# A five-unit decoder layer on one core: PSUM banks copied out at once, convolution taps tied to each pair, two operations moved to VectorE, first loads reordered

## The chip, the core and the metric

The kernel runs on one core of a Trainium2 chip. The core has a matrix engine (TensorE, PE in the rows, with its weight loads as PEld), VectorE (DVE), ScalarE (ACT), GpSimd (POOL) and SyncE (SP), whose queue (SPq) issues every DMA of this kernel. Each engine takes its own instructions in the order in which the program lists them. The metric is device time of the whole program in microseconds.

## What is computed

One mixer layer over 4096 rows of 1024 numbers, all in fp32:

```
h    = layer_norm(x)
proj = h @ w_in                          # 1024 -> 3072, split in six parts of 512
a    = a_val * sigmoid(a_gate)
y_a  = silu(layer_norm(causal_depthwise_conv(a, 31 taps))) * silu(a_z)
v    = layer_norm(gelu(b_v));  sv = masked 128x128 W_s per head @ v + b_s
y_b  = gelu(b_u) * sv * silu(b_z)
mix  = concat(y_a, y_b) @ w_out          # 1024 -> 1024
h    = layer_norm(2**0.25 * h + mix)
out  = h + sigmoid(h @ w_gate + b) * (p @ w_ple)
```

## The kernel before

**Units and pairs.** The five matrix products of 1024 by 1024 are five *units*, run one after the other. Unit 0 makes `a`, unit 1 makes `u` and `v` and the spatial mix, unit 2 makes the two `silu` gates, unit 3 is the output projection with its residual and norm, unit 4 the gate and the result. A unit walks over 16 *pairs* of 128 rows each. What a unit leaves for a later one goes to DRAM (`hT`, `qD`, `aD`, `cD`, `uD`, `ybD`, `azD`, `zT`).

**One pair.** A pair is a 2 by 2 block product done with seven products in place of eight (`group`, L320; the order is 1, 5, 6, 3, 7, 2, 4). A product is 12 matmuls of 512 columns, because each operand is split in a high and a low part and three of the four combinations are kept (`product`, L304). So a pair has 84 such matmuls. The partial sums live in four PSUM banks of one buffer each, with tags A, B, D and E. Bank B is used by products 1, 6 and 7 one after the other; between them an instruction reads it (`plus`, L323, on ACT in units 0 to 2 and on DVE at L327 or L329 in units 3 and 4). Product 2 adds to bank A and product 4 to bank D, and both banks are first written by a `plus`: `pa` and `pd`. What a pair makes in halves `c12` and `c22` comes from `tt(to12, ...)` (L345) and `tt(to22, ...)` (L350) on DVE. Two more banks (tag S) serve transposes, two (tag acc) the convolution.

**Left operands.** They are made one pair ahead: in units 0, 3 and 4 from 16 transposes and seven splits (`rows_left`, L242), in units 1 and 2 from the `qD` kept by unit 0 (`left_kept`, L232). A split (`left`, L226) is a copy on ACT and a subtraction on POOL or DVE.

**Weights.** Seven weight operands of a unit are split by `split_weight` (L168) on ACT and DVE. Those of units 1 to 4 are made in DRAM (`twD`) during the unit before by `combos` (L176: loads, 16 POOL subtractions, stores) and loaded in that unit's last pair (`load_operands`, L406), since their 14 buffers are those of the running unit.

**Background work.** Between products, `between(i)` (i from 0 to 5) advances five lists of generators: left operands (`bg`), weights (`bg_w`), rows two pairs ahead (`bg_x`), the work after a pair (`bg_post`) and the convolution (`bg_conv`). The convolution has 16 pieces (4 blocks of 1024 rows by 4 channel groups), each of 47 DVE instructions, the *taps* (L379, L381, L387, L390), 752 in all. A block becomes available when unit 0 has made its four pairs; `y_rows` (unit 3's input) needs it. The number of taps per `between` is the last argument of `unit`: 2 in unit 0, 3 in units 1 and 2, 2 in unit 3.

**The order on an engine.** The program is written in this order, but a planner then lays out each engine's list from planned times, and may put an instruction of a background list ahead of where it is written when its engine would be free. The order is fixed at build time.

**Buffers.** SBUF tiles of up to 8 KB per partition share one pool of seven (`big`): rows, staged weights, `hr`, `y`, `cz`, `z`, and the broadcast rows `eb`, `prow`, `gb`. A new tile waits for one of the seven.

**Where the change lies.** In unit 3 the norm of a pair (`body_d`, L687) reads bank A and bank D by `moments` (L147, L148, DVE), takes the power and the bias on POOL (`scale_bias`, L154) and only then is the bank read for the last time:

```python
for dst, src in ((z[:, j, 0:C], ps), (z[:, j, C:], z[:, j, C:])):
    act(dst, src, ID, scale=mv[:, 0, 1:2], bias=nb[:, 0:1])
```

`y_rows` (L636) does the same with a bank of tag S. `norm_v` (L573, unit 1) scales and shifts `v` with two POOL operations, L580 and L581. `first_operands` (L200) issues the eight loads of the first weights after the first rows are normed; `gb`, the gate's bias (L738), is loaded after unit 3 has ended.

## Time and profile before

| what | value |
|---|---|
| median of 3 runs | 2052.64 us (2052.59 to 2060.61) |
| the profiled execution: its own time | 2056.51 us |
| the profiled execution: its span | 2054.8 us, mean granted clock 0.955 |
| units 0 to 4, from the ends of their last products | 414.4, 375.6, 331.2, 481.9 and 451.8 us |

Times in the rows are microseconds from the first instruction unless marked ns. The granted clock is TensorE's, as a share of 2.4 GHz. In rows of single instructions, what stands in brackets is how long the engine stood idle before it and what ended that. In rows of stretches, each engine has its busy time and its number of instructions.

### The profile page before, as it was taken

The page shows a single profiled execution, that of the slowest core. Times are in us where ns is not written, and L with a number is a line of the kernel's source. Part 1 is how long each engine was busy: PE and PEld are TensorE (multiplying, and loading weights), DVE is VectorE, ACT ScalarE, POOL GpSimd, SP SyncE. Part 2 cuts the span into 40 slices and gives each one's busy share as a digit, 9 for nine tenths or more (in the row PEclk, how much of TensorE's full clock was granted, in tenths as well). Part 3 has the DMA queues.
Part 4 walks back from the last instruction along what each step waited for, and adds up shares of the span by engine and source line. Part 5 has one row for each costly group of instructions (what it writes and reads, how often), then busy time and mean ns, then how long its engine had stood idle before and what let it go on. Part 6 is the DMA issues. An engine that isn't in the chain of part 4 may idle for free.

```text
span 2054.8 us, 24446 instructions
## 1 busy us (share of the span) xinstructions
PE 1857.2 (90%) x8322; PEld 1504.2 (73%) x8322; DVE 1354.9 (66%) x2139; ACT 869.9 (42%) x1406; POOL 1361.2 (66%) x1110
## 2 busy tenths in 40 slices
PE   4798999988899998999999787889888699999999
PEld 3687888867687886788887566667666477888887
DVE  7648999999999999884004434444446565666665
ACT  4654555653354545444446323333333422223331
POOL 2869877468888887886665666655556545566661
PEclk8999999999999999999999988999998899999999
DMA  6579676766634436995457475333334422222221
GB/s 221 195 257 321 236 245 205 251 210 210 217 117 145 127 121 222 325 353 201 174 190 273 157 253 208 125 122 144 130 126 153 170 93 85 86 87 88 88 93 57
DMA packets 184926, 363.63 MB, mean 177 GB/s; under 512 B 49633, under 2 KB 74209, under 8 KB 177121
## 3 DMA queue, kind: packets, MB, share of 16 engines
q1 hardware_dynamic: 184800, 362.07, 51.1%
q8 instruction: 66, 1.08, 0.2%
q14 instruction: 60, 0.48, 0.1%
HBM read 211.02 MB, written 150.99 MB: 176 GB/s over the span
## 4 chain that ended last, share of the span: by engine, by line
PE 63%; DMA 10%; DVE 9%; POOL 8%; ACT 4%; issue 4%; SPq 0%; DVEq 0%; POOLq 0%; ACTq 0%
PE pb L309 9%; PE pb L310 8%; PE pb L311 8%; PE pe L309 5%; PE pe L310 5%; PE pe L311 5%; PE pp L764 4%; PE tp L254 3%; PE pa L309 3%; PE pa L310 3%; PE pa L311 3%; POOL alo L229 2%; PE pd L309 2%; PE pd L311 2%; PE pd L310 2%
## 5 line engine op out<-in xcount | busy, mean ns | idle before, releaser
L309 PE MATMUL pb<-whi,ahi 128*128 128x512 f32 x960 | 404.4, 421 | 96.8 <-DVE pa L329 48.1
L229 POOL TENSOR_TENSOR alo<-s,ahi 128x512 fp32r<-128x512 f32 x192 | 261.5, 1372 | 322.5 <-ACT ahi L228 311.8
L310 PE MATMUL pb<-wlo,ahi 128*128 128x512 f32 x960 | 394.6, 411 | 1.1 <-DVE wlo L173 1.1
L311 PE MATMUL pb<-whi,alo 128*128 128x512 f32 x960 | 393.7, 410 | 1.7 <-DVE alo L229 1.7
L309 PEld LDWEIGHTS pb<-whi,ahi 128*128 128x128 f32 x960 | 192.1, 200 | 147.9 <-DVE pa L329 52.4
L309 PE MATMUL pe<-whi,ahi 128*128 128x512 f32 x640 | 257.9, 403 | 9.9 <-ACT ahi L228 5.4
L311 PE MATMUL pe<-whi,alo 128*128 128x512 f32 x640 | 255.9, 400 | 6.4 <-POOL alo L229 6.4
L310 PE MATMUL pe<-wlo,ahi 128*128 128x512 f32 x640 | 254.0, 397 | 5.8 <-DVE wlo L173 5.8
L229 POOL TENSOR_TENSOR alo<-qa,ahi 128x512 fp32r<-128x512 f32 x128 | 165.5, 1308 | 96.9 <-ACT ahi L228 95.5
L311 PEld LDWEIGHTS pb<-whi,alo 128*128 128x128 f32 x960 | 191.6, 200 | 44.9 <-DVE alo L229 2.4
L310 PEld LDWEIGHTS pb<-wlo,ahi 128*128 128x128 f32 x960 | 192.1, 200 | 41.5 <-DVE wlo L173 3.7
L381 DVE SCALAR_TENSOR_TENSOR acc<-ca,cs_sb,acc 128x512 f32<-128x512 f32 x240 | 180.2, 751 | 4.6
L390 DVE SCALAR_TENSOR_TENSOR acc<-ca,cw_sb,acc 128x512 f32<-128x512 f32 x240 | 179.2, 747 | 0.2
L228 ACT ACTIVATE ahi<-s 128x512 fp32r<-128x512 f32 x192 | 120.1, 630 | 125.4 <-DVE s L281 60.1
L387 DVE SCALAR_TENSOR_TENSOR acc<-zy,cw_sb,acc 128x512 f32<-128x512 f32 x224 | 167.1, 746 | 1.2
L229 DVE TENSOR_TENSOR alo<-tp,ahi 128x512 fp32r<-128x512 f32 x144 | 98.7, 685 | 95.5 <-ACT ahi L228 89.9
L309 PEld LDWEIGHTS pe<-whi,ahi 128*128 128x128 f32 x640 | 122.3, 191 | 37.8 <-ACT ahi L228 7.9
L229 POOL TENSOR_TENSOR alo<-qb,ahi 128x512 fp32r<-128x512 f32 x96 | 126.4, 1328 | 32.3 <-ACT ahi L228 31.0
L311 PEld LDWEIGHTS pe<-whi,alo 128*128 128x128 f32 x640 | 122.3, 191 | 33.4 <-POOL alo L229 8.4
L310 PEld LDWEIGHTS pe<-wlo,ahi 128*128 128x128 f32 x640 | 122.3, 191 | 32.2 <-DVE wlo L173 8.3
L309 PE MATMUL pd<-whi,ahi 128*128 128x512 f32 x320 | 129.5, 405 | 5.1 <-ACT pd L325 5.1
L228 ACT ACTIVATE ahi<-tp 128x512 fp32r<-128x512 f32 x144 | 84.8, 590 | 105.7 <-PE tp L254 104.8
(149 smaller groups left out, 4001.7 us busy)
## 6 DMA issues: line engine op xcount, KB each, us to landing
qa<-qD SPq DMA_DIRECT2D x32, 1024.0 KB, 6.6
twD<-bq SPq DMA_DIRECT2D x112, 256.0 KB, 5.4
wst<-twD SPq DMA_DIRECT2D x28, 1024.0 KB, 5.8
qb<-qD SPq DMA_DIRECT2D x32, 768.0 KB, 6.9
xr<-in_x SPq DMA_DIRECT2D x32, 512.0 KB, 5.0
hT<-xr SPq DMA_DIRECT2D x32, 512.0 KB, 3.0
qD<-s SPq DMA_DIRECT2D x64, 256.0 KB, 3.2
bq<-in_wq SPq DMA_DIRECT2D x64, 256.0 KB, 5.3
```

The costliest lines, as they stand in the source:

```text
L228: act(hi, src, ID)
L229: eng.tensor_tensor(lo, src, hi.bitcast(F32), op=SUB)
L254: nc.tensor.transpose(out=tp[:, kk * P : (kk + 1) * P], in_=rows[:, j, k * P : (k + 1) * P], identity=ident,)
L309: nc.tensor.matmul(ps, lhsT=ah[:, k, :], rhs=wh[:, k, :], start=start and k == 0, stop=False, **kw)
L310: nc.tensor.matmul(ps, lhsT=ah[:, k, :], rhs=wl[:, k, :], start=False, stop=False, **kw)
L311: nc.tensor.matmul(ps, lhsT=al[:, k, :], rhs=wh[:, k, :], start=False, stop=k == 3, **kw)
L381: stt(even, src, w, even, op0=MUL, op1=ADD)
L387: stt(dst, src, cw_sb[:, ct, 2 * k + 1 : 2 * k + 2], odd if k else even, op0=MUL, op1=ADD)
L390: stt(src if k == NE - 1 else even, src, cw_sb[:, ct, 2 * k : 2 * k + 1], even, op0=MUL, op1=ADD,)
L764: nc.tensor.matmul(pp, lhsT=l[:, k, ts], rhs=r[:, k, cs], start=k == 0 and l is ph and r is wp_hi, stop=k == 1 and l is pl,)
```

## The change

The diff has these parts.

1. Unit 3's norm: ACT copies banks A and D to `z` as soon as they are done, and a new generator `z_out` makes the moments, the scale and the store from SBUF in the next pair, as `bg_post` steps.
2. The same in `y_rows`: the transposed convolution is copied out of its bank first, the two norms share one `scale_bias` call.
3. `group` records in `anchor` the last of L345 and L350; convolution taps are advanced only at `between(2)` and `between(3)`, and `tc.issue_after` keeps each tap behind that instruction in DVE's list. Quotas go from 2, 3, 3, 2 at six places to 6, 6, 10, 5 at two places.
4. Unit 1's scale and shift of `v` go from POOL (`ptt`) to DVE (`tt`).
5. The loads of the first weights are issued before the first rows are normed; `gb` is loaded in unit 3's last pair.

```diff
--- before.py
+++ after.py
@@ -197,13 +197,16 @@
             dma(twD[u][ROW[4]][:, c], q[:, 2])
             yield
 
-    def first_operands(W):
+    def load_first():
         stg = {}
         for ij in ((0, 0), (0, 1), (1, 1), (1, 0)):
             stg[ij] = big([P, 4, C], "wst")
             for c in range(2):
                 cs = slice(2 * c, 2 * c + 2)
                 dma(stg[ij][:, cs], wq[0][ij][:, cs])
+        return stg
+
+    def first_operands(W, stg):
         b11, b12, b22, b21 = (stg[ij] for ij in ((0, 0), (0, 1), (1, 1), (1, 0)))
 
         def sub(dst, a, b):
@@ -316,6 +319,8 @@
         nc.gpsimd.memset(z.bitcast(F32), 0.0)
         for tag in ("A", "D"):
             nc.tensor.matmul(pbank(tag, "seed"), lhsT=z[:, 0, :], rhs=flat(z), start=True, stop=True)
+
+    anchor = []
 
     def group(L, W, add, to12, to22, between, scale=None):
 
@@ -342,12 +347,12 @@
         plus(u2, pb, 1)
         between(1)
         product(pe, 3, L, W, False)
-        tt(to12, pe, u2, op=ADD)
+        anchor[:] = [tt(to12, pe, u2, op=ADD)]
         between(2)
         product(pb, 7, L, W, False)
         pd = pbank("D", "pd")
         plus(pd, pb, 2)
-        tt(to22, pb, s5, op=ADD)
+        anchor[:] = [tt(to22, pb, s5, op=ADD)]
         between(3)
         product(pa, 2, L, W, False)
         between(4)
@@ -437,7 +442,9 @@
                     bg_w.step(2 if i == 5 else 1)
                 else:
                     bg_w.step(1)
-                bg_conv.step(conv_quota)
+                if i in (2, 3):
+                    with tc.issue_after(anchor[0].ins):
+                        bg_conv.step(conv_quota)
 
             body(p, L, W, between)
             bg.drain()
@@ -474,13 +481,14 @@
     load_x(0)
     W = {}
     eb = broadcast(erow, 2, "eb")
+    stg = load_first()
     for _ in h_rows(0, nc.vector):
         pass
     open_banks()
     L = {}
     for _ in rows_left(L, X.pop(0), qD[0]):
         pass
-    first_operands(W)
+    first_operands(W, stg)
     dma(cw_sb, cw)
     nc.vector.tensor_copy(cs_sb, cw_sb[:, :, 0::2])
     tt(cs_sb[:, :, 0 : NE - 1], cs_sb[:, :, 0 : NE - 1], cw_sb[:, :, 1::2], op=ADD)
@@ -529,7 +537,7 @@
         bg_post.drain()
         bg_post.add(a_out(p, (c12, c22)))
 
-    L, W = unit(0, L, W, left_a, lambda L: left_kept(0, L), body_a, 2, 2)
+    L, W = unit(0, L, W, left_a, lambda L: left_kept(0, L), body_a, 2, 6)
     bg_post.drain()
 
 
@@ -577,8 +585,8 @@
             moments([v], mv[:, 0, :])
             nb = scale_bias(mv)
             act(v, v, ID, scale=mv[:, 0, 1:2], bias=nb[:, 0:1])
-            ptt(v, v, sgb[0][:, 0], op=MUL)
-            ptt(v, v, sgb[1][:, 0], op=ADD)
+            tt(v, v, sgb[0][:, 0], op=MUL)
+            tt(v, v, sgb[1][:, 0], op=ADD)
             act(V["h"][:, i], v, ID)
             ptt(V["l"][:, i], v, V["h"][:, i].bitcast(F32), op=SUB)
 
@@ -598,7 +606,7 @@
         if p % 2 == 1:
             bg_post.add(mix(p // 2, V["g"], V["h"], V["l"]))
 
-    L, W = unit(1, L, W, left_kept, lambda L: left_kept(0, L), body_b, 2, 3)
+    L, W = unit(1, L, W, left_kept, lambda L: left_kept(0, L), body_b, 2, 6)
     bg_post.drain()
 
 
@@ -646,11 +654,16 @@
                     in_=cc[:, ct, j],
                     identity=ident,
                 )
-            mv = mvtile(1)
-            moments([tp], mv[:, 0, :])
-            nb = scale_bias(mv)
+            act(y[:, j, 0:C], tp, ID)
+        yield
+        mv = mvtile(2)
+        for j in (1, 0):
+            moments([y[:, j, 0:C]], mv[:, j, :])
+        nb = scale_bias(mv)
+        yield
+        for j in (1, 0):
             ya = y[:, j, 0:C]
-            act(ya, tp, ID, scale=mv[:, 0, 1:2], bias=nb[:, 0:1])
+            act(ya, ya, ID, scale=mv[:, j, 1:2], bias=nb[:, j : j + 1])
             yield
             ptt(ya, ya, cgb[0][:, 0], op=MUL)
             ptt(ya, ya, cgb[1][:, 0], op=ADD)
@@ -678,11 +691,24 @@
             cgb.append(broadcast(crow[i : i + 1, :], 1, "cgb", utile))
         yield from first_y(L)
 
-    L, W = unit(2, L, W, left_kept, first_y_, body_c, 2, 3)
+    L, W = unit(2, L, W, left_kept, first_y_, body_c, 2, 10)
 
 
     for _ in y_rows(1):
         pass
+
+    def z_out(p, z):
+        mv = mvtile(2)
+        for j in range(2):
+            moments([z[:, j, 0:C], z[:, j, C:]], mv[:, j, :])
+            yield
+        nb = scale_bias(mv)
+        yield
+        yield
+        for j in range(2):
+            act(z[:, j], z[:, j], ID, scale=mv[:, j, 1:2], bias=nb[:, j : j + 1])
+            dma(zT[p][j], z[:, j])
+            yield
 
     def body_d(p, L, W, between):
         if p == 1:
@@ -698,12 +724,9 @@
             z[:, 0, C:], z[:, 1, C:], between, scale=ALPHA,
         )
         for j, ps in ((0, pa), (1, pd)):
-            mv = mvtile(1)
-            moments([ps, z[:, j, C:]], mv[:, 0, :])
-            nb = scale_bias(mv)
-            for dst, src in ((z[:, j, 0:C], ps), (z[:, j, C:], z[:, j, C:])):
-                act(dst, src, ID, scale=mv[:, 0, 1:2], bias=nb[:, 0:1])
-            dma(zT[p][j], z[:, j])
+            act(z[:, j, 0:C], ps, ID)
+        bg_post.drain()
+        bg_post.add(z_out(p, z))
 
     Z = {}
 
@@ -719,14 +742,16 @@
             ptt(Z[p][:, j], Z[p][:, j], pb_[0][:, 1], op=ADD)
             yield
 
-    pb_ = []
+    pb_, last_const = [], []
 
     def first_z(L):
         pb_.append(broadcast(prow, 2, "prow"))
+        last_const.append(broadcast(grow, 1, "gb")[:, 0])
         yield from z_rows(0)
         yield from rows_left(L, Z[0])
 
-    L, W = unit(3, L, W, left_y, first_z, body_d, 2, 2)
+    L, W = unit(3, L, W, left_y, first_z, body_d, 2, 5)
+    bg_post.drain()
 
 
     wp_hi, wp_lo = big([P, 2, D], "wph", F32R), big([P, 2, D], "wpl", F32R)
@@ -735,7 +760,7 @@
     for k in range(2):
         act(wp_hi[:, k], wps[:, k], ID)
         tt(wp_lo[:, k], wps[:, k], wp_hi[:, k].bitcast(F32), op=SUB)
-    gb = broadcast(grow, 1, "gb")[:, 0]
+    gb = last_const[0]
     for _ in z_rows(1):
         pass
```

## Rows read from the trace of the kernel before

**Rows 1.** The profile's first table: each engine's busy time, share of the span and number of instructions.

```profile
PE 1857.2 (90%) x8322; PEld 1504.2 (73%) x8322; DVE 1354.9 (66%) x2139; ACT 869.9 (42%) x1406; POOL 1361.2 (66%) x1110
```

**Rows 2.** Busy time by stretch: unit 0's first pair, the rest of unit 0, then units 1, 2, 3 and 4. Columns: the stretch, its length, each engine's busy time and number of instructions, granted clock, DMA share, GB/s.

```profile
0.00:76.00 76.00, 39.00 (x123) 26.96 (x124) 56.25 (x71) 35.99 (x46) 30.32 (x28) 0.84 0.57 201
76.00:414.00 338.00, 332.13 (x1612) 273.22 (x1612) 276.84 (x447) 194.71 (x321) 255.68 (x185) 0.99 0.73 252
414.00:790.00 376.00, 342.16 (x1510) 277.31 (x1508) 355.65 (x599) 178.99 (x309) 320.89 (x298) 0.97 0.50 162
790.00:1121.00 331.00, 320.36 (x1385) 261.25 (x1385) 164.32 (x225) 155.74 (x249) 231.12 (x178) 0.97 0.71 251
1121.00:1603.00 482.00, 399.54 (x1743) 319.06 (x1741) 229.69 (x442) 171.73 (x270) 280.40 (x297) 0.90 0.46 163
1603.00:2055.00 452.00, 423.97 (x1957) 346.39 (x1955) 272.16 (x360) 132.77 (x216) 242.84 (x127) 0.97 0.26 90
```

**Rows 3.** The same for the convolution's taps on DVE alone, in units 0, 1 and 2 (no other stretch has any). Columns: the stretch, its length, DVE busy time in taps and their number, granted clock, DMA share, GB/s.

```profile
76.00:414.00 338.00, 138.50 (x193) 0.99 0.73 252
414.00:790.00 376.00, 286.12 (x405) 0.97 0.50 162
790.00:1121.00 331.00, 108.32 (x154) 0.97 0.71 251
```

**Rows 4.** Busy time by stretch as in rows 2, finer: unit 1's pairs 0 to 5 and 6 to 15; unit 2's pairs 7 to 14 (to 1102); unit 3's pairs 0 to 4 and 5 to 14; one pair of unit 0 (pair 10); one pair of unit 3 (pair 7).

```profile
414.00:575.00 161.00, 135.50 (x561) 107.04 (x560) 152.62 (x246) 71.47 (x121) 131.32 (x120) 0.93 0.64 207
575.00:790.00 215.00, 206.66 (x951) 170.28 (x949) 203.03 (x355) 107.52 (x189) 189.56 (x179) 1.00 0.40 129
950.00:1102.00 152.00, 152.00 (x676) 126.00 (x675) 13.96 (x24) 67.07 (x112) 93.32 (x73) 1.00 0.52 186
1121.00:1290.00 169.00, 132.85 (x564) 103.34 (x562) 76.39 (x145) 58.68 (x93) 106.92 (x110) 0.89 0.62 211
1290.00:1576.00 286.00, 243.01 (x1080) 196.63 (x1079) 131.01 (x273) 102.81 (x163) 159.12 (x181) 0.92 0.37 133
284.00:306.00 22.00, 22.00 (x110) 18.19 (x109) 19.98 (x33) 12.71 (x21) 17.95 (x15) 1.00 0.72 246
1348.00:1376.00 28.00, 23.70 (x109) 19.20 (x108) 12.88 (x27) 10.03 (x16) 15.56 (x19) 0.94 0.35 129
```

**Rows 5.** Waits over the whole run: who waited for what, the total in us, how often, the longest. L579 is an instruction of unit 1 alone, L329 of unit 3 alone.

```profile
ACT v L579 <- POOL nb L161: 44.5, 16, 7.9
...
PE pb L309 <- DVE pa L329: 48.1, 16, 3.6
```

**Rows 6.** The instructions in order of time around the start of unit 3's pair 10: start, duration, engine, line, operation. The first row reads bank A for the moments; the last four are single matmuls of the product after the wait.

```profile
1437.53 0.68 DVE L147 BATCH_NORM_STATS2 st<-pa 128x6 f32<-128x512 f32 x1
...
1441.91 0.74 POOL L161 TENSOR_SCALAR nb<-mv 128x1 f32<-128x1 f32 x3
...
1443.49 0.77 ACT L705 ACTIVATE z<-pa,nb,mv 128x512 f32<-128x512 f32 x1
...
1444.29 0.70 DVE L329 SCALAR_TENSOR_TENSOR pa<-hr,pb 128x512 f32<-128x512 f32 x1 [2.03 <-ACT z L705]
...
1445.04 0.79 PE L309 MATMUL pb<-whi,ahi 128*128 128x512 f32 x1 [3.61 <-DVE pa L329]
...
1446.06 0.63 PE L311 MATMUL pb<-whi,alo 128*128 128x512 f32 x1
1446.49 0.63 PE L309 MATMUL pb<-whi,ahi 128*128 128x512 f32 x1
...
1448.41 0.39 PE L311 MATMUL pb<-whi,alo 128*128 128x512 f32 x1
1448.64 0.39 PE L309 MATMUL pb<-whi,ahi 128*128 128x512 f32 x1
```

**Rows 7.** Groups of instructions of one line and shape over the whole run: number, busy time in us, mean ns of one, idle time of the engine before them.

```profile
L580 POOL TENSOR_TENSOR v<-v,sgb 128x512 f32<-128x512 f32 x32 | 42.2, 1329 | 3.9 <-ACT v L579 3.6
L769 DVE TENSOR_TENSOR zr<-zr,c 128x512 f32<-128x512 f32 x32 | 53.9, 1683 | 1.1
L769 DVE TENSOR_TENSOR zr<-zr,sg 128x512 f32<-128x512 f32 x32 | 22.1, 692 | 1.1
L259 ACT ACTIVATE zq<-tp 128x512 f32<-128x512 f32 x64 | 38.0, 595 | 45.6 <-PE tp L254 43.0 <-DMA aD<-at 2.4
L468 ACT ACTIVATE xr<-xr,nb,mv 128x1024 f32<-128x1024 f32 x32 | 38.5, 1239 | 17.3 <-POOL nb L161 17.1
```

**Rows 8.** A piece of the chain of work that ended last, inside unit 1's pair 3: start, length, what.

```profile
505.33 8.28 DMA twD<-bq
```

**Rows 9.** The instructions in order of time around unit 4's first pair, columns as in rows 6.

```profile
1619.24 0.38 SPq L416 DMA_DIRECT2D gb<-in_grow  x1
...
1623.75 0.70 DVE L327 TENSOR_TENSOR pa<-pb,gb 128x512 f32<-128x512 f32 x1 [1.62 <-DMA gb<-in_grow]
...
1624.60 0.76 PE L309 MATMUL pb<-whi,ahi 128*128 128x512 f32 x1 [18.73 <-DVE pa L327]
```

**Rows 10.** The same at the program's start.

```profile
14.72 1.46 SPq L471 DMA_DIRECT2D hT<-xr  x2
...
16.22 2.39 SPq L206 DMA_DIRECT2D wst<-in_wq  x4
...
21.42 1.06 ACT L172 ACTIVATE whi<-wst 128x1024 fp32r<-128x1024 f32 x1 [0.92 <-DMA wst<-in_wq]
```

## The prediction, made before the change was run

> **What bounds the kernel now.** I read the engine table first. PE is busy for 90% of the span and no other engine for more than 66% [rows 1], so the time is made of PE's work and of the places where PE waits or runs slowly. The stretches by unit show where those are [rows 2]: the granted clock is 0.97 to 0.99 in most units, 0.84 in the first pair and 0.90 in unit 3. The finer stretches give a yardstick [rows 4]. A pair of unit 0 with 84 matmuls and 24 transposes takes 22.0 us with PE busy throughout at clock 1.00. A pair of unit 3 has the same 84 matmuls and 24 transposes (16 in `rows_left`, 8 in `y_rows`) and takes 28 us, PE busy for 23.7 of them at clock 0.94. A pair of unit 2 (84 matmuls alone) takes 152 / 8 = 19.0. So unit 3 has 6 us a pair to lose, and unit 2's later pairs have nothing.
>
> The instructions around the start of a unit 3 pair say what it waits for [rows 6]. Product 6 starts at 1445.04 after 3.61 us of idle PE, behind the DVE instruction that writes bank A. That one waited for ACT's last read of bank A, at 1443.49, which waited for the bias from POOL (1441.91), which comes from moments that DVE began at 1437.53. The whole run has 16 such waits, 48.1 us [rows 5]. Behind the wait, matmuls start 0.43 us apart (1446.06, 1446.49), later 0.23 apart (1448.41, 1448.64): the lower and the upper of TensorE's two levels, 1.2 and 2.4 GHz [rows 6]. Of the product's 12 matmuls about seven run slowly, 7 x 0.20 = 1.4 us more.
>
> **Part 1, banks copied at once.** Two ACT copies from PSUM of 0.595 us [rows 7] take the place of two bank reads of 0.77 [rows 6]; the norm then works on 1024 columns from SBUF at 1.24 each [rows 7]. ACT gains about 0.6 us a pair, and is busy for 10.0 of 28 [rows 4]: hidden by idle ACT. Bank A is now free about a microsecond after product 2, one product before the pair's end, and its next writer comes after the next pair's product 1. What is late next? DVE must still read bank B between products, with one product of 2.7 us (12 x 0.23) as slack for an instruction of 0.70: enough. The moments stay DVE's four per pair, the two stores of `zT` stay on SP's queue, some microseconds later or earlier; behind them stand the loads of `hr` and `y` for later pairs. `z` itself is kept into the next pair, as it was before (its norm ended 10 us into the next pair [rows 6]).
>
> Pairs 5 to 14 take 286 us now [rows 4]. I set them at 22.5 each, the yardstick and 0.5 for what is left: 225, a gain of 61. Pairs 0 to 4 take 169, with POOL busy for 107 [rows 4] because `combos` adds its 16 subtractions there and its loads compete for the seven buffers. There I count the wait and the slow matmuls alone, 5 x (2.5 + 1.4), 20. Its bounds are 0 (buffers set the pace) and 169 - 5 x 22 = 59.
>
> **Part 2, `y_rows`.** The same move frees a transpose bank earlier. Two ACT copies more per pair, 2 x 0.6, into idle ACT. I price it at nothing beside the yardstick; with its cover gone it costs 1.2 us a pair, 19 in all.
>
> **Part 3, taps.** Taps are 193, 405 and 154 in units 0, 1 and 2, at 138.50 / 193 = 0.72 us each [rows 3]. The new quotas allow 12, 12, 20 and 10 a pair: at most 144 in unit 0 (12 pairs have some), 192 in unit 1, 320 in unit 2, and 96 are left for unit 3's first ten pairs; `y_rows` asks for their block in pair 10, so none is forced. DVE per pair after: unit 1 has (355.65 - 286.12) / 16 = 4.3 [rows 2, 3] + 12 x 0.71 = 12.8; unit 2 has 13.96 / 8 = 1.7 [rows 4] + 20 x 0.71 = 15.9, of 19.0; unit 3 has 12.9 [rows 4] + 10 x 0.72 = 20.1, of 22. It fits everywhere, narrowly in unit 3. Each `between` puts a block of 6 x 0.72 = 4.3, 10 x 0.72 = 7.2 or 5 x 0.72 = 3.6 us behind `to12` or `to22`. In unit 2, `to22` may stand behind 7.2 us of taps: 0.7 + 7.2 + 0.7 = 8.6 after product 3, while PE needs bank B again three products (8.2 us) later. That is up to 0.4 a pair if the planner doesn't interleave them; 16 x 0.3 = 5 lost. At the entry to unit 3, where before no tap ran, 20 + 10 taps meet the weight splits: 5 more lost (bounds 0 and 30 x 0.72 = 22). The entry to unit 2 (331 us for the unit against 16 x 19 = 304 [rows 2]) has fewer taps before it than now: 5 gained (bounds 0 and 27). Unit 0 after its first pair takes 338 us [rows 2] against 15 x 22 = 330 and has 49 taps fewer: 4 gained (bounds 0 and 8). Sum: -1.
>
> **Part 4, scale and shift on DVE.** POOL loses 64 operations of 1.33 us [rows 7], 5.3 a pair; DVE gains 4 of about 0.69 (the fast form in [rows 7]), 2.8 a pair, 15.6 with the taps. Unit 1's first six pairs take 161 us with POOL busy for 131 and DVE for 153; the last ten take 215, 21.5 each [rows 4]. At that pace six take 129, a bound of 32. But transfers are in the chain there too, one of 8.28 us for a `twD` store [rows 8], and nothing in the change shortens them. I take 20. The last ten, with DVE no longer full (203 of 215), gain 5, of a bound of 215 - 10 x 20.4 = 11 (19.0, and half of 24 matmuls of half the columns, 24 x 0.115 / 2 = 1.4). Unit 1: 25. The change adds a wait: DVE's `tt` waits for ACT's normed `v`, and that waited for POOL 16 times, up to 7.9 us [rows 5]. Behind it on DVE stand taps, the spatial mix and `to22`, for which PE's bank B waits.
>
> What DVE pays for such an operation is not one number. L769 adds two SBUF tiles of 128x512 into SBUF; in its two forms it takes 692 or 1683 ns on the mean [rows 7]. At the upper value the 64 moved operations cost 64 x 1.68 = 108 us in place of 44. The Trainium skill, GPSIMD Engine Reference, section Specifications, says that GpSimd and VectorE share SBUF interfaces and contend when a VectorE instruction has two SBUF inputs, as the moved ones have. By that rule the sum for unit 1 would be the one with 1.68, a rival below; the trace agrees as far as the spread of L769 goes.
>
> **Part 5, loads.** The first weights are issued at 16.22, behind the store of `hT` at 14.72 [rows 10]; four issues took 2.4 us, so all eight now pass before 10 us and delay no store. DVE is busy for 56 of the first 76 us [rows 2] and splits weights from 22 us on [rows 10]; some 5 us of that can now go into its idle time before. The first rows still gate PE. 5 gained, bounds 0 and 10. `gb` is issued at 1619.24, and PE waits 18.73 us for the instruction that reads it [rows 9]. Loaded a pair earlier, this goes down to other work of that entry (unit 4's last weights): 15, bounds 5 and 19.
>
> **Sum.** 61 + 20 - 1 + 25 + 5 + 15 = 125, against the profiled execution's own 2056.51: 1931.5. That execution lies 3.9 above the median of the runs, so I say 1930. With the upper bounds of the entries of units 1, 3 and 4, the loads and unit 0, 39 + 12 + 6 + 4 + 5 + 4 = 70 more, it would be 1860. A measurement of this kernel tells 0.5%, about 10 us, from no change.
>
> **The rivals.**
> - *More than that.* If the buffers and POOL don't set the pace in unit 3's first pairs and unit 1's first pairs, both go to the yardstick: 39 + 18 more, 1873. For it: POOL's 107 of 169 leaves room. Against it: the `twD` store in the chain [rows 8].
> - *DVE becomes the bound.* With 20.1 of 22 us in unit 3's first ten pairs, blocks of taps may hold back the reads of bank B: ten pairs take 4 us more than set above, 40 lost, and unit 1's later pairs gain nothing, 5: 1975. Against it: unit 0's pair is at 22.0 with DVE busy for 20.0 [rows 4].
> - *Moved operations at the slow price.* 64 us more DVE work, 4 a pair: 19.6 with the taps, about the length of a pair. Unit 1 gains 10 in place of 25: 1945. The two forms of L769 speak for it, one each way. The Trainium skill's rule named in part 4 (GPSIMD Engine Reference, Specifications) would have it so whenever POOL is busy.
> - *Slower than before.* Taps in a block keep PE from bank B in each of the 44 pairs of units 0 to 2 that have them. It decides once it costs more than 125 / 44 = 2.8 us a pair; at unit 3's price of 3.6 + 1.4 a wait it is 220: 2150. For it: blocks up to 7.2 us. Against it: the slack of 8.2 us, and unit 2's 154 taps, all in its seven pairs before 950 (later pairs show 1.7 us of DVE), so 22 in each [rows 3, 4].
> - *The copy does not come at once.* It stands in ACT's list behind other copies or the norm, and bank A is as late as now: the 81 of unit 3 are gone, 2010.
>
> **How the numbers follow.** Forecast (1900 to 1960) 0.50, more 0.17, DVE bound 0.16, slow price 0.07, slower 0.05, late copy 0.05. All but *slower* end more than 10 us under the time before. With a little for a mixture of the bad ones: faster 0.92, same 0.03, slower 0.05. The range takes in the forecast and the cases from 1873 to 1975, with a margin of some units of the last sums: 1868 to 1990; outside are the last two cases, 0.10.
>
> **What would show it.** Waits of PE for L329 near zero and unit 3's later pairs at 22 to 23 us at clock 1.00; taps spread as counted, and none before its pair's L345; unit 1's POOL at some 15 us a pair; no idle of 18 us in unit 4's first pair; the first weights landing before 20 us. It is wrong if a wait for DVE (L345, L350) stands ahead of PE in unit 2, or if unit 3's early pairs stay over 30 us.

## The result, and the profile after

The changed kernel takes 2002.08 us (median of four runs, 2001.10 to 2003.35), beside 2054.19 for the kernel before on the same chip: a ratio of 0.9741, 95% interval 0.9718 to 0.9764. The profiled execution took 2001.87 us, with a span of 2000.2. It is faster, as forecast, by 52 us where I had said 125, and the time lies above my range of 1868 to 1990.

After the change lines are shifted: the `plus` of units 3 and 4 on DVE is L334 and L332 (before L329 and L327), on ACT L330 (L325); the matmuls are L312 to L314, the two `tt` are L350 and L355 (L345 and L350), the left split is L231 and L232. `y_rows` copies at L657, norms at L666 and has its POOL operations at L668, L669 and L671. A tap is one of L384, L386, L392, L395.

The page's engine table:

```profile
PE 1831.2 (92%) x8322; PEld 1484.9 (74%) x8322; DVE 1397.0 (70%) x2171; ACT 902.1 (45%) x1438; POOL 1268.2 (63%) x1014
```

Against [rows 1], POOL has 96 instructions and 93 us less; DVE and ACT have 32 instructions more each, and 42 and 32 us. Stretches by unit, columns as in [rows 2]:

```profile
0.00:73.00 73.00, 35.35 (x123) 26.19 (x124) 55.83 (x71) 36.79 (x47) 30.12 (x29) 0.81 0.59 215
73.00:411.00 338.00, 331.38 (x1613) 272.86 (x1612) 240.66 (x391) 195.96 (x320) 250.60 (x181) 0.99 0.72 249
411.00:756.00 345.00, 331.08 (x1509) 272.55 (x1507) 263.53 (x448) 180.74 (x308) 247.38 (x228) 0.99 0.50 165
756.00:1080.00 324.00, 315.02 (x1387) 257.55 (x1388) 268.63 (x386) 157.20 (x252) 227.29 (x181) 0.99 0.76 264
1080.00:1547.00 467.00, 388.47 (x1726) 304.75 (x1725) 291.97 (x515) 196.01 (x297) 274.80 (x271) 0.93 0.49 169
1547.00:2000.00 453.00, 429.94 (x1972) 350.97 (x1970) 276.43 (x365) 135.36 (x218) 238.06 (x127) 0.98 0.26 94
```

From the ends of the last products, units 0 to 3 take 411.2, 344.6, 324.1 and 466.9 us, and the rest 453.4: 3, 31, 7 and 15 less than before and 2 more. Unit 1 gave 31 where I had put 25. Unit 3, where I had put 76 us of the gain, gave 15. Its pairs 0 to 4, 5 to 9 and 10 to 14:

```profile
1080.00:1258.00 178.00, 135.93 (x564) 105.72 (x563) 114.98 (x195) 66.14 (x102) 106.45 (x100) 0.87 0.63 208
1258.00:1400.00 142.00, 118.96 (x541) 93.20 (x541) 92.95 (x174) 59.41 (x90) 77.11 (x82) 0.96 0.38 130
1400.00:1524.00 124.00, 114.03 (x539) 90.08 (x538) 64.54 (x129) 59.15 (x91) 76.16 (x82) 1.00 0.44 157
```

The last five are at 24.7 each and clock 1.00. The five before them take 28.4 each (28.6 before the change), though DVE is busy for only 93 of 142 us. What differs is the taps. The same view as [rows 3], taps alone, in units 0, 1, 2 and in unit 3 up to pair 9:

```profile
73.00:411.00 338.00, 97.52 (x136) 0.99 0.72 249
411.00:756.00 345.00, 139.57 (x194) 0.99 0.50 165
756.00:1080.00 324.00, 218.92 (x313) 0.99 0.76 264
1080.00:1400.00 320.00, 78.06 (x109) 0.91 0.52 173
```

PE's waits in unit 3 (who for what, total, times, longest):

```profile
PE tp L257 <- POOL y L671: 37.6, 15, 8.5
PE pe L312 <- ACT ahi L231: 9.2, 10, 1.4
PE pb L312 <- DVE u L334: 8.9, 15, 0.7
...
PE pb L312 <- DVE pa L334: 0.7, 1, 0.7
```

The wait of [rows 5] for bank A has gone from 48.1 us to 0.7. In its place PE waits for the next pair's left operand: for `y`, the last thing that `y_rows` writes. In pairs 5 to 9 alone (1258 to 1400 us) this wait is

```profile
PE tp L257 <- POOL y L671: 12.8, 5, 3.3
```

Pair 7, with 1.35 us the shortest of these five waits, shows how `y` comes late (timeline: start, duration, engine, line; idle time ahead and its releaser in brackets):

```profile
1308.79 1.54 DVE L386 SCALAR_TENSOR_TENSOR acc<-ca,cs_sb,acc 128x512 f32<-128x512 f32 x2
1309.46 1.09 ACT L657 ACTIVATE y<-tc 128x512 f32<-128x512 f32 x2 [1.71 <-PE tc L652]
1310.24 1.28 DVE L147 BATCH_NORM_STATS2 st<-y 128x6 f32<-128x512 f32 x2
...
1314.71 0.70 DVE L392 SCALAR_TENSOR_TENSOR acc<-zy,cw_sb,acc 128x512 f32<-128x512 f32 x1
1315.32 0.75 DVE L395 SCALAR_TENSOR_TENSOR acc<-ca,cw_sb,acc 128x512 f32<-128x512 f32 x1
1315.97 0.16 DVE L158 TENSOR_SCALAR mv<-mv 128x2 f32<-128x2 f32 x1
1316.22 0.70 POOL L159 TENSOR_TENSOR mv<-mv,nhalf 128x2 f32<-128x2 f32 x1 [6.46 <-DVE mv L158]
...
1318.72 2.55 POOL L668 TENSOR_TENSOR y<-y,cgb 128x512 f32<-128x512 f32 x2
...
1321.89 2.55 POOL L669 TENSOR_TENSOR y<-y,cgb 128x512 f32<-128x512 f32 x2
...
1324.87 2.52 POOL L671 TENSOR_TENSOR y<-y,cz 128x512 f32<-128x512 f32 x2
...
1327.45 1.09 PE L257 MATMUL tp<-ident,y 128*128 128x128 f32 x8 [1.35 <-POOL y L671]
```

From the copy of the bank to PE's transpose is 18 us of one chain. POOL stood idle for 6.46 us ahead of its power, because DVE's list has taps and `z`'s moments between and behind `y`'s moments; and POOL takes both rows at each step (x2), so the first row waits for the second. PE starts on `y` 0.1 us after the second row's last multiplication.

### The profile page after: what moved, and what is told of

Its sections match the earlier page's. It is cut to its first block, busy times and chain, and to the rows that moved or that the text cites. A ratio compares the mean times of both kernels' runs of the same rounds, so it can differ in the third digit from the quotient of the medians.

```text
span 2000.2 us, 24365 instructions
## 1 busy us (share of the span) xinstructions
PE 1831.2 (92%) x8322; PEld 1484.9 (74%) x8322; DVE 1397.0 (70%) x2171; ACT 902.1 (45%) x1438; POOL 1268.2 (63%) x1014
## 3 DMA queue, kind: packets, MB, share of 16 engines
q1 hardware_dynamic: 184800, 362.07, 52.4%
## 5 line engine op out<-in xcount | busy, mean ns | idle before, releaser
L232 POOL TENSOR_TENSOR alo<-s,ahi 128x512 fp32r<-128x512 f32 x192 | 263.7, 1383 | 354.5 <-ACT ahi L231 346.7
L312 PE MATMUL pb<-whi,ahi 128*128 128x512 f32 x960 | 394.2, 411 | 32.9 <-ACT pa L330 11.0
L314 PE MATMUL pb<-whi,alo 128*128 128x512 f32 x960 | 385.4, 401 | 3.5 <-DVE alo L232 3.5
L313 PE MATMUL pb<-wlo,ahi 128*128 128x512 f32 x960 | 385.0, 401 | 2.4 <-DVE wlo L173 2.4
L312 PE MATMUL pe<-whi,ahi 128*128 128x512 f32 x640 | 255.6, 399 | 23.4 <-ACT ahi L231 13.8
L314 PE MATMUL pe<-whi,alo 128*128 128x512 f32 x640 | 255.2, 399 | 7.8 <-POOL alo L232 7.5
L312 PEld LDWEIGHTS pb<-whi,ahi 128*128 128x128 f32 x960 | 186.3, 194 | 84.7 <-ACT pa L330 14.8
L314 PEld LDWEIGHTS pb<-whi,alo 128*128 128x128 f32 x960 | 186.2, 194 | 44.0 <-DVE alo L232 3.7
L313 PEld LDWEIGHTS pb<-wlo,ahi 128*128 128x128 f32 x960 | 186.9, 195 | 40.3 <-DVE wlo L173 3.7
L232 POOL TENSOR_TENSOR alo<-qa,ahi 128x512 fp32r<-128x512 f32 x128 | 169.8, 1340 | 62.7 <-ACT ahi L231 62.4
L231 ACT ACTIVATE ahi<-s 128x512 fp32r<-128x512 f32 x192 | 120.1, 631 | 171.1 <-DVE s L284 79.9
L386 DVE SCALAR_TENSOR_TENSOR acc<-ca,cs_sb,acc 128x512 f32<-128x512 f32 x240 | 180.0, 750 | 4.4
L395 DVE SCALAR_TENSOR_TENSOR acc<-ca,cw_sb,acc 128x512 f32<-128x512 f32 x240 | 179.0, 746 | 0.0
L392 DVE SCALAR_TENSOR_TENSOR acc<-zy,cw_sb,acc 128x512 f32<-128x512 f32 x224 | 167.2, 746 | 0.8
L274 DVE TENSOR_TENSOR s<-tp,a 128x512 f32<-128x512 f32 x32 | 22.1, 692 | 201.7 <-ACT a L268 127.0
L312 PEld LDWEIGHTS pe<-whi,ahi 128*128 128x128 f32 x640 | 121.9, 190 | 53.4 <-ACT ahi L231 26.0
L232 POOL TENSOR_TENSOR alo<-qb,ahi 128x512 fp32r<-128x512 f32 x96 | 126.3, 1323 | 49.8 <-ACT ahi L231 43.5
L314 PEld LDWEIGHTS pe<-whi,alo 128*128 128x128 f32 x640 | 121.3, 189 | 35.7 <-POOL alo L232 11.5
L232 DVE TENSOR_TENSOR alo<-tp,ahi 128x512 fp32r<-128x512 f32 x144 | 96.9, 682 | 70.8 <-ACT ahi L231 69.4
L312 PE MATMUL pd<-whi,ahi 128*128 128x512 f32 x320 | 130.4, 408 | 3.1 <-ACT pd L330 2.5
```

The costliest lines, as they stand in the source:

```text
L231: act(hi, src, ID)
L232: eng.tensor_tensor(lo, src, hi.bitcast(F32), op=SUB)
L274: tt(s1, t22, a21, op=ADD)
L312: nc.tensor.matmul(ps, lhsT=ah[:, k, :], rhs=wh[:, k, :], start=start and k == 0, stop=False, **kw)
L313: nc.tensor.matmul(ps, lhsT=ah[:, k, :], rhs=wl[:, k, :], start=False, stop=False, **kw)
L314: nc.tensor.matmul(ps, lhsT=al[:, k, :], rhs=wh[:, k, :], start=False, stop=k == 3, **kw)
```

## The experiments

Times in us: median and ratio to the kernel before with its 95% interval (the ratio is to runs on the same chip, whose medians were 2051.9 to 2054.3), then from each run's profile unit 1, unit 3, and unit 3's first pair, pairs 1 to 4 and pairs 5 to 9.

| kernel | median | ratio | unit 1 | unit 3 | pair 0 | 1–4 | 5–9 |
|---|---|---|---|---|---|---|---|
| before | 2054 | 1 | 375.6 | 481.9 | 39.5 | 129.9 | 143.1 |
| after | 2002.1 | 0.9741 (0.9718–0.9764) | 344.6 | 466.9 | 52.4 | 125.9 | 142.0 |
| e1_taps_early | 1981.4 | 0.9646 (0.9627–0.9665) | 358.6 | 433.4 | 47.4 | 115.6 | 123.8 |
| e8_taps_old | 1994.6 | 0.9718 (0.9690–0.9747) | 376.5 | 432.8 | 47.2 | 115.5 | 123.6 |
| e2_old_y | 1986.9 | 0.9675 (0.9660–0.9690) | 344.9 | 450.6 | 53.2 | 120.9 | 134.3 |
| e4_z_alone | 1997.9 | 0.9733 (0.9714–0.9753) | 373.1 | 419.8 | 38.5 | 120.4 | 119.0 |
| e3_old_z | 2009.5 | 0.9798 (0.9770–0.9825) | 344.3 | 477.9 | 52.4 | 124.7 | 145.2 |
| c2_early_oldy | 1974.1 | 0.9616 (0.9595–0.9636) | 358.9 | 418.6 | 38.5 | 119.8 | 119.4 |
| c3_varied_oldy | 1976.5 | 0.9631 (0.9605–0.9657) | 354.9 | 422.2 | 41.7 | 120.5 | 119.1 |
| c4_unit2_oldy | 1984.2 | 0.9666 (0.9620–0.9711) | 356.4 | 427.2 | 46.9 | 120.5 | 119.0 |
| e7_v_alone | 2044.2 | 0.9963 (0.9946–0.9981) | 376.2 | 477.8 | 38.5 | 129.1 | 143.1 |
| e9_v_on_pool | 2029.1 | 0.9890 (0.9872–0.9908) | 365.1 | 476.5 | 55.0 | 127.3 | 145.6 |
| e5_gb_late | 2004.4 | 0.9765 (0.9743–0.9786) | 345.0 | 470.9 | 54.8 | 126.2 | 146.8 |
| e6_z1_first | 2006.2 | 0.9774 (0.9755–0.9794) | 344.6 | 473.5 | 55.1 | 126.2 | 146.3 |

My theory on seeing the result: taps in unit 3 take the place of the wait. The rival: the joined norm of `y_rows` does.

**e1_taps_early**: as after, but all taps end before unit 2's last pair (the ends of the three `unit` calls, side by side).

```diff
-body_a, 2, 6)   -body_b, 2, 6)   -body_c, 2, 10)
+body_a, 2, 8)   +body_b, 2, 8)   +body_c, 2, 11)
```

> The changed kernel, but with tap quotas 8, 8 and 11 in units 0, 1 and 2 in place of 6, 6 and 10: all 752 taps are issued by unit 2's pair 13, none in its last pair or in unit 3. The taps theory (unit 3's first ten pairs are slow because 96 taps stand in DVE's list ahead of the moments and the bank reads, and unit 3's first pair is long because taps stand between the weight splits) expects unit 3's pairs 5 to 9 at 24.8 us each like pairs 10 to 14 of the changed kernel, in place of 28.4 (18 less), its first pair at about 40 in place of 52.4 (12 less), pairs 1 to 4 some 5 less in sum: 1967 against 2002. The y theory (the two norms of y_rows are joined in one step and there are seven steps in place of five, so the row that is needed first comes late) expects pairs 5 to 9 within 1 us of 28.4 and at most the first pair's 12: 1990 to 2002.

The theory holds behind the first pair; that pair stays at 47, where it expected 40. The rival's forecast, pairs 5 to 9 within 1 us of 28.4, failed; whether the first pair is the rival's, c2 below will tell. Unit 3 falls by 33.5 us: 5 in the first pair, 10 in pairs 1 to 4, 18 in pairs 5 to 9. Stretch of pairs 5 to 9, columns as above:

```profile
1265.00:1388.00 123.00, 113.25 (x539) 89.53 (x538) 62.58 (x125) 58.16 (x90) 73.98 (x81) 1.00 0.42 150
```

DVE does 30 us less than in the 142 us above, those of the taps; ACT and POOL do about as much as there, so the taps hardly stretch their work. PE reaches clock 1.00, and its busy time falls by 5.7 us. Its wait for `y` falls by 11, from 12.8 to 1.8 in the five pairs. The two make 17 of the 18. The gain in the whole is less, since unit 1 takes 14 more.

**e8_taps_old**: as after, but with part 3 undone (quotas 2, 3, 3, 2 at six places, no `issue_after`).

```diff
-                if i in (2, 3):
-                    with tc.issue_after(anchor[0].ins):
-                        bg_conv.step(conv_quota)
+                bg_conv.step(conv_quota)
```

> The changed kernel with part 3 undone: taps in every step with quotas 2, 3, 3 and 2, tied to nothing, so that they lie in units 0, 1 and the first pairs of unit 2 as before. The taps theory expects unit 3 to gain what taps cost there, 35 us, and unit 1 and 2 to lose some 15 to 25 of their 38 gained, because DVE is full there again: 1982 to 1992. If tying the taps is worth what units 1 and 2 gained, and taps cost nothing in unit 3, the time is 2025 or more.

Unit 3 is e1's within a microsecond (no taps there either), unit 1 loses all that it had gained, 32 us, where I expected units 1 and 2 to lose 15 to 25 (the time is 3 above my range). So part 3 as a whole, 32 gained in unit 1 and 34 lost in unit 3, costs some 7 us.

**e2_old_y**: as after, but each row of `y_rows` is normed out of its transpose bank as before.

```diff
-            act(y[:, j, 0:C], tp, ID)
-        yield
-        mv = mvtile(2)
-        for j in (1, 0):
-            moments([y[:, j, 0:C]], mv[:, j, :])
-        nb = scale_bias(mv)
-        yield
-        for j in (1, 0):
+            mv = mvtile(1)
+            moments([tp], mv[:, 0, :])
+            nb = scale_bias(mv)
             ya = y[:, j, 0:C]
-            act(ya, ya, ID, scale=mv[:, j, 1:2], bias=nb[:, j : j + 1])
+            act(ya, tp, ID, scale=mv[:, 0, 1:2], bias=nb[:, 0:1])
```

> The changed kernel with part 2 undone: y_rows takes moments, scale and norm from the transpose bank, one row after the other, as before. The y theory expects PE's waits for the last multiplication of y to go: unit 3's pairs 5 to 9 from 28.4 to about 25.5, pairs 10 to 14 from 24.8 to 24, pairs 0 to 4 some 10 less in sum: about 1975. The taps theory expects pairs 5 to 9 to stay within 1.5 us of 28.4, and the time between 1995 and 2012.

15 us faster than after. The rival is right too, though not in the size that it forecast (pairs 5 to 9 at 26.9 each for 25.5, the time 12 above its 1975); the taps theory alone, which put the time at 1995 or more, is not enough. Both hold.

**e4_z_alone**: the kernel before with part 1 and nothing else (`z_out` as in the change).

```diff
-            mv = mvtile(1)
-            moments([ps, z[:, j, C:]], mv[:, 0, :])
...
-            dma(zT[p][j], z[:, j])
+            act(z[:, j, 0:C], ps, ID)
+        bg_post.drain()
+        bg_post.add(z_out(p, z))
```

> The kernel before with one part of the change alone: unit 3's banks copied out at once and z_out in the next pair. Taps are as before, none in unit 3. If copying the banks is what takes away the wait for bank A and taps are what gave it back, unit 3's pairs 5 to 15 go from 28.4 to about 24.8 and pairs 0 to 4 lose some 10 in sum: 50 less than before, 2004. If the copy itself brings a new wait (the buffers that z now holds, the norm in ACT's list), pairs 5 to 15 stay at 27 or more: 2035 or more.

Unit 3 falls by 62 us. This one part gives the time of the whole change. Its steady pairs are 23.8, not 22.5; PE waits some 1.5 us in each, here in pair 5 (timeline; L271 is the first `s` of the left operands, L329 the `u` that reads bank B behind product 6; on PE's list products 2 and 3 come next, and then product 7, whose first matmul is the last row):

```profile
1285.03 0.69 DVE L271 TENSOR_TENSOR s<-tp,a 128x512 f32<-128x512 f32 x1 [5.11 <-PE tp L254]
1285.63 0.68 DVE L329 SCALAR_TENSOR_TENSOR u<-hr,pb 128x512 f32<-128x512 f32 x1
...
1286.37 0.50 PE L309 MATMUL pb<-whi,ahi 128*128 128x512 f32 x1 [1.48 <-DVE u L329]
```

DVE is idle for 5.11 us, with an instruction at the head of its list that needs transposes which PE makes behind products 2 and 3 (at 1284.29). The read of bank B, for which PE waits, stands behind it, though product 6 had ended at 1278.96. In unit 3 of the kernel before PE waited for this `u` once, 1.7 us; here 15 times, 25.3 us.

**e3_old_z**: as after, with part 1 undone: e4's diff the other way round.

> The changed kernel with unit 3's norm as before: banks A and D are read by the moments and released by the norm. If part 1 is what takes the waits for bank A away, they come back, 40 us or more over unit 3, and its steady pairs 10 to 14 go from 24.7 to 28 or more: 2020 to 2045. If with taps in unit 3 the norm's place matters less because PE waits for y anyway, pairs 5 to 9 stay at 28 and the time is 2010 to 2020.

Only 7 us slower than after by the medians, 12 by the ratios, 11 in unit 3; pairs 5 to 9 stay at 29. Inside the whole change part 1 is worth about 10, alone 56: the other parts wait in the same pairs.

**c2_early_oldy**: the two diffs of e1 and e2 together.

> The changed kernel with the quotas of e1 (8, 8, 11: no tap in unit 2's last pair and in unit 3) and y_rows as before the change. If taps and the new y_rows each cost what the first runs show (34 us in unit 3; 9 in its first pair and 1.0 in each steady pair, less 5 in pairs 1 to 4), unit 3 comes down to 418 to 424, as in the kernel with part 1 alone: steady pairs at 23.8, the first at 39; unit 1 stays at 358: 1965 to 1972. If the first pair's length comes from the taps alone, it stays at 47 and the time at 1975 or more.

The lowest median of all, 2 us above the range that I had given it. Its unit 3 is that of e4. Pairs 5 to 9, columns as above, and PE's only wait of size from 1262 to 1400:

```profile
1251.00:1371.00 120.00, 112.52 (x545) 90.82 (x544) 63.31 (x130) 53.72 (x80) 78.46 (x87) 1.00 0.44 154
```

```profile
PE pb L312 <- DVE u L334: 8.9, 6, 1.5
```

With the old `y_rows` PE starts on the first row of `y` while the second is still being made (timeline, pair 5):

```profile
1257.48 1.31 POOL L666 TENSOR_TENSOR y<-y,cz 128x512 f32<-128x512 f32 x1
...
1261.74 0.60 PE L257 MATMUL tp<-ident,y 128*128 128x128 f32 x4
...
1265.79 1.27 POOL L666 TENSOR_TENSOR y<-y,cz 128x512 f32<-128x512 f32 x1 [0.74 <-ACT y L665]
```

It starts 5.3 us before the second row's last multiplication ends; in e1, as in after, 0.1 us behind it.

So unit 3 goes up in steps: 418.6 with part 1 and neither of the others (c2); +14.8 with the joined `y_rows` (e1, of which 8.9 in the first pair, where PE waits 8.09 us for `y`); +33.5 with taps (after). Where `y_rows` is the old one, taps cost 32.0 (e2 against c2). Over the unit the two costs add up, in the first pair they don't: 38.5 with neither, 47.4 with the joined `y_rows`, 53.2 with taps, 52.4 with both.

**e7_v_alone** and **e9_v_on_pool**: the kernel before with part 4 alone, and after without part 4 (the same two lines the other way round).

```diff
-            ptt(v, v, sgb[0][:, 0], op=MUL)
-            ptt(v, v, sgb[1][:, 0], op=ADD)
+            tt(v, v, sgb[0][:, 0], op=MUL)
+            tt(v, v, sgb[1][:, 0], op=ADD)
```

> The kernel before with the scale and shift of v moved to VectorE and nothing else. If POOL sets unit 1's pace, the unit goes from 376 to about 350 and the time to 2030. If DVE, full of taps there, sets it, the unit stays at 370 to 385: 2048 to 2063.

> The changed kernel with the scale and shift of v left on POOL: part 3 without part 4. If taking taps out of unit 1 is what gained its 31 us, the unit stays at 345 to 350 and the time at 2000 to 2008. If the gain needs both, because POOL with 320 us of work is next in line once DVE has room, the unit is at 358 or more and the time at 2015 or more.

Unit 1 takes 376.2 with part 4 alone (no gain: what e7 gains lies in units 2 to 4, and 64 of unit 1's taps have moved into unit 2 there), 365.1 with the rest alone, 344.6 with both. Its first six and last ten pairs, in e7 to within 1.5 us, then in e9 (columns as in [rows 2]):

```profile
414.00:575.00 161.00, 133.47 (x555) 105.85 (x555) 154.27 (x240) 70.35 (x119) 108.42 (x97) 0.90 0.62 203
575.00:790.00 215.00, 207.78 (x955) 171.44 (x953) 208.06 (x356) 108.25 (x189) 148.57 (x140) 0.99 0.39 129
```

```profile
411.60:568.30 156.70, 136.76 (x562) 108.57 (x561) 90.31 (x152) 71.49 (x121) 130.76 (x117) 0.92 0.59 194
568.30:776.70 208.40, 204.49 (x949) 169.23 (x947) 124.35 (x239) 109.16 (x188) 181.52 (x172) 1.00 0.37 119
```

In e7 DVE is full (362 of 376 us). In e9 it has room, and POOL is the busier, 312 of 365; in after both have room, 263 and 247 of 345. Taking load off one engine brought nothing or 10 us until the other's went too. That the full engine is the cause is read from these busy times; no run shows it apart.

**e5_gb_late** (as after, but `gb` loaded after unit 3) and **e6_z1_first** (as after, but `z_rows(1)` asked for ahead of the `w_ple` load).

```diff
 # e5
-        last_const.append(broadcast(grow, 1, "gb")[:, 0])
...
-    gb = last_const[0]
+    gb = broadcast(grow, 1, "gb")[:, 0]
 # e6
+    for _ in z_rows(1):
+        pass
     wp_hi, wp_lo = big([P, 2, D], "wph", F32R), big([P, 2, D], "wpl", F32R)
...
-    for _ in z_rows(1):
-        pass
```

> The changed kernel with gb loaded after unit 3 again. The moved-wait theory (with gb there early, PE stops a little later at the transposes of the next rows, whose load waits for one of the seven buffers) expects unit 4's first pair between 42 and 48 us, as it is with gb early (46.1), and the time within 5 of 2002. The theory that early gb is worth its 18.7 us and something else took it expects 2010 to 2020.

> The changed kernel with unit 4's second rows (z_rows for pair 1) asked for before the weights of the last small product, not after them. The moved-wait theory expects the load at 1567.9 and POOL's four operations of 2.35 us behind it to move forward by most of the 12.3 us that PE waits for them: unit 4's first pair at 34 to 38 in place of 46.1, the time about 1992. If no buffer is free before the last pair's z is stored, whatever stands first, nothing moves: within 3 of 2002.

Unit 4's first pair takes 46.1 in after, 47.4 in e5, 42.5 before. Timeline of that pair in after:

```profile
1556.59 0.76 PE L312 MATMUL pb<-whi,ahi 128*128 128x512 f32 x1 [3.89 <-DVE pa L332]
1573.05 4.64 POOL L741 TENSOR_TENSOR zr<-zr,prow 128x1024 f32<-128x1024 f32 x2 [12.89 <-DMA zr<-zT]
1580.03 1.97 PE L257 MATMUL tp<-ident,zr 128*128 128x128 f32 x8 [12.25 <-POOL zr L742]
```

and in e5:

```profile
1573.72 0.76 PE L312 MATMUL pb<-whi,ahi 128*128 128x512 f32 x1 [14.78 <-DVE pa L332]
1585.61 1.09 PE L257 MATMUL tp<-ident,zr 128*128 128x128 f32 x8 [1.24 <-POOL zr L742]
```

The theory of a wait that only moved holds; what I expected of e6 (34 to 38 us for this pair) didn't come: it takes 44.4. With `gb` early PE waits for the rows of pair 1 instead, whose load is issued at 1567.88, with that of pair 2 right behind. In e6 the load of pair 1 comes at 1563.46, that of pair 2 at 1581.08, and later pairs give back the 6 us that the first two gain. What holds these loads, the seven buffers by the argument, isn't shown.

**c3_varied_oldy** (c2 with quotas 9; 4 in unit 1's first six pairs, then 8; 12) and **c4_unit2_oldy** (c2 with quotas 9, 6, 13).

```diff
 # c3
-body_a, 2, 8)   -body_b, 2, 8)                             -body_c, 2, 11)
+body_a, 2, 9)   +body_b, 2, lambda p: 4 if p < 6 else 8)   +body_c, 2, 12)
 # c4
+body_a, 2, 9)   +body_b, 2, 6)                             +body_c, 2, 13)
```

> The same with 18 taps a pair in unit 0, 8 in unit 1's first six pairs and 16 in its others, 24 in unit 2, so that all end in unit 2's pair 13. Unit 1's length has followed its taps (194 taps 344.6 us, 259 taps 358.6, 343 taps 376.5), most of it in its first six pairs: 139 us with 12 taps a pair, 152 with 16, so with 8 they should take 130 to 139 and the unit about 342. Unit 2 must hold 24 x 0.71 + 1.7 = 18.7 us of DVE in 19.0; if that fits without a wait: 1948 to 1955. If unit 2 or unit 0 slows (over 22.5 or 20 us a pair): 1960 or more.

> The change with the transposed rows normed as before and the quotas at 9, 6 and 13: about 192 taps in unit 0, 194 in unit 1 (as many as the change has there) and the other 366 in unit 2, none in unit 3. In unit 2 that is 26 taps a pair, 26 x 0.70 = 18.3 us, with 1.7 us of other work 20 us of VectorE a pair where the pair takes 19.0. If a tap costs by what it fills (VectorE's time), unit 1 is back at 345 and unit 2's fourteen pairs lose about 1 us each, 337: 1974 - 14 + 15 = about 1975. If it costs only by the order, unit 2 stays at 323 and the whole is 1974 - 14 = about 1960. If unit 1's first pairs don't depend on the number of taps at all (at 4 a place they took 151 us, at 6 a place 139), unit 1 stays at 355 to 359 and the whole is 1974 to 1990.

Neither beats c2, and c3 is a plain miss: 1976 for 1948 to 1955, unit 1 at 355 for 342. c4 lies in the last of its three cases. c4 answers one thing: pairs 6 to 13 of unit 2 with 24 taps each (190 in all), columns as in [rows 2]:

```profile
902.80:1055.20 152.40, 152.40 (x674) 126.19 (x673) 141.43 (x206) 66.58 (x113) 104.87 (x83) 1.00 0.63 214
```

DVE is busy for 93% and PE loses nothing, at 19.05 a pair. The last two pairs have 36 taps, among the weight splits of the entry, where c2 has 6: unit 2's last pair takes 22.2 in place of c2's 18.3, unit 3's first 46.9 in place of 38.5. In c4 unit 1's first six pairs take 151 us as in e1 and c3, with 210 taps in that unit; in every kernel with quotas 6, 6, 10 and part 4 they take 139, with 194, and e1 has 259. So the number of unit 1's taps isn't what sets them; in those six pairs c3 has 72, after 79. What goes with the length is unit 0's quota, 6 in all five kernels at 139 and 8 or 9 in the four at 151 to 152, but no run tries that alone, and the cause stays open.

## Why the prediction was right and wrong, point by point

**Part 3 in unit 3, the step that failed most.** I summed DVE's busy time, 20.1 of 22 us, and concluded "It fits everywhere, narrowly in unit 3"; for the entry I took 5. Measured (after against e1): 33.5 in unit 3 (5.0 of it in the first pair, 28.5 in pairs 1 to 9, 3.2 each), and 2.8 in the pair ahead. The entry's size was about right beside the joined `y_rows` (with the old one the first pair loses 14.7, e2 against c2); the fit was the wrong test. DVE wasn't full, 93 of 142 us. A tap of 0.75 us costs in unit 3 because DVE's list is in order and part of a chain (moments, power, scale, `y`, transpose) for which PE waits. That the taps cost it is shown by e1; that their place in the list does it, and not their number, is read from pair 7's timeline, and no run puts the same taps elsewhere in that list. In unit 2, where the next pair's left operands come without DVE, 24 taps a pair at 93% cost nothing (c4). But a chain through DVE's list isn't enough by itself. Unit 0's left operands come through it too, and there eight pairs of the kernel before (7 to 14, columns as in [rows 2]) lose next to nothing with DVE at 96%:

```profile
218.00:394.00 176.00, 175.60 (x865) 145.06 (x866) 169.54 (x278) 102.08 (x172) 125.98 (x92) 1.00 0.65 224
```

What differs is the slack: in these pairs POOL's last write to the rows ends 0.5 to 7.7 us ahead of PE's transposes, in the last six of them 4.1 or more; in unit 3 of after it is 0.1 us. The rival *DVE becomes the bound* had the place and about the size, 4 us in each of ten pairs, but by another cause, the reads of bank B: in after PE waits for `u` 0.7 us at most. Its 1975 kept nearly all the other gains. My own sign of being wrong, unit 3's early pairs over 30 us, came: the first five take 178.3 us, 9 more than before.

**Part 2, priced at nothing.** Measured 14.8 us in unit 3 (c2 to e1), in the whole 15 (e2 to after) or 7 (c2 to e1, where unit 4 takes 5 less). I counted two copies on ACT, "with its cover gone it costs 1.2 us a pair". What costs is order: both rows are held until the last is normed, as PE's start 0.1 us behind the second row shows, and `y_rows` takes seven steps in place of five, of which `between` advances six in a pair. Which of these two weighs more isn't separated. Steady pairs lose 0.9 (24.7 against 23.8), the first 8.9. I looked at which engine is busy, not at when `y` is needed.

**Part 1.** The mechanism was right: in e4 the wait for bank A's writer falls from 48.1 to 5.3 us, and pairs 5 to 9 run at clock 1.00. Its size: 81 forecast, 62 measured alone (58 in pairs 0 to 14: 10.5 in the first five for 20, 47.4 in the next ten for 61). My yardstick of 22.0 was a pair of unit 0, whose reads of bank B are on ACT; in unit 3 they are on DVE, one of them behind `s`, and some 1.5 us of waiting a pair are left. The question "what is late next" I answered with a duration (0.70 us in a slack of 2.7), not with the list.

**`gb`, 15 with bounds 5 and 19.** Nothing gained: after and e5 agree within 2 us. The 18.73 us of [rows 9] covered a second wait, for `zr`, that ends as late. Unit 4's first pair is 3.6 longer than before the change, in e5 too; why stays open.

**Parts 3 and 4 in unit 1.** Forecast 25, measured 31, and only both together give it. *Moved operations at the slow price* didn't come: the moved ones (groups of after: number, busy time, mean ns),

```profile
L589 DVE TENSOR_TENSOR v<-v,sgb 128x512 f32<-128x512 f32 x32 | 29.3, 922 | 0.4
L588 DVE TENSOR_TENSOR v<-v,sgb 128x512 f32<-128x512 f32 x32 | 25.7, 806 | 24.5 <-ACT v L587 24.5
```

took 55 us in all, for 44 forecast and 108 at the slow price, and DVE had room.

**The small ones.** Loads: the first weight split starts at 11.90 in place of 21.42, and the first pair is 2.8 shorter (forecast 5). Unit 0's other pairs didn't change (forecast 4). Unit 2 gained 7 (forecast 5 at the entry less 5 in its pairs): the loss of 0.3 a pair from taps ahead of `to22` didn't come. Nothing of *slower* came either.

**The sum.** Unit 3 short by 61 (18 of part 1, 28 of taps, 15 of `y_rows`), `gb` by 15 and what unit 4 lost by 2, unit 0 by 6, less 6 in unit 1 and 7 in unit 2: 71 of the 125 missing, which leaves the 54.6 by which the span fell. My range summed parts as if each kept its gain beside the others; e3 and e4 show one part worth about 10 or 56.

## What to carry to other kernels

Before filling an engine's free time with background work, ask not how full it is but how early the things are ready that the bottleneck takes from its list in that stage. Here the filler cost nothing at 93% where no left operand came through the list (unit 2), nor at 96% where the rows mostly lay ready 4 us or more ahead (unit 0), and 3 us a pair at 65% where they came just in time (unit 3). A yardstick taken from another stage holds only if the same engine does the same reads there. And a part that takes a wait away should be tried alone: the best version here keeps most of the change and drops the joined norm and the taps of one unit (1974 us in place of 2002).

## What the runs showed of the hardware

At the entry to unit 3 POOL's operations stretch while DVE splits weights, but not beside taps (timeline of after; L173 reads two SBUF tiles, a tap one and a PSUM bank):

```profile
1081.58 2.35 DVE L173 TENSOR_TENSOR wlo<-wst,whi 128x1024 fp32r<-128x1024 f32 x2
1081.60 3.46 POOL L232 TENSOR_TENSOR alo<-s,ahi 128x512 fp32r<-128x512 f32 x1 [7.13 <-ACT ahi L231]
...
1096.28 3.79 POOL L232 TENSOR_TENSOR alo<-s,ahi 128x512 fp32r<-128x512 f32 x3 [5.00 <-ACT ahi L231]
```

One L232 takes 3.46 us beside splits, and three take 1.26 each beside taps and reads of PSUM; a split takes 1.2 alone (1076.79) and up to 1.9 beside POOL (1073.64 in the same timeline). The Trainium skill, GPSIMD Engine Reference, section Specifications, says that the two engines share SBUF interfaces and contend when a VectorE instruction has two SBUF inputs; the trace agrees, and POOL is the one that loses more here.
